# Scan of a hybrid flow step: attention's four scaled copies queued on ScalarE in written order, and the block inverse's conversions kept apart on ScalarE

## The chip, the cores and the metric

The kernel runs on one core of one Trainium2 chip, in one launch. The metric is device time in microseconds; the time before is the median of three runs. All instructions of the core are issued on five engines, each in its own order: TensorE (PE, with its weight loads PEld), VectorE (DVE), ScalarE (ACT), GpSimd (POOL) and SyncE (SP). Semaphores tie the engines together. DMAs are issued from the queues of SP, ACT and POOL.

## The reference, cut to what matters

One layer of a backbone for 128 context tokens and 2048 sample tokens, `D_MODEL` 1024. One input projection feeds three branches of 512 columns (a gated DeltaNet scan in both directions, a spatial gating MLP, a Fourier mix); each branch is gated, projected and merged.

```python
# the scan, chunk after chunk, forwards and backwards (H_A = 4 heads of 128)
m   = eye + beta * (k k^T) * dec_strict          # unit lower triangular, one per chunk and head
sol = solve_triangular(m, [beta v, beta exp(gam) k])
def step(s, inp):
    u = u0 - w @ s
    o = qg @ s + qk @ u                           # attention's output
    s = gl * s + kd^T @ u
    return s, o
# the branches
br  = stack([norm(o) * silu(z_a), sgu(u_b, v_b) * silu(z_b), fourier(x_c) * silu(z_c)])
merged = sum(sigmoid(gates) * (br @ w_branch)); y = rmsnorm(h + gate * (merged @ w_out))
```

## The kernel before, in words

All products are done in fp16 pairs (a high half and a low half, three matmuls for one product), so PE has most of the work: large products over 512 columns (`gemm_T`, `gemm_N`, line 250 with `xh`, `xl`, `whi`, `wlo`), and the small products of the scan, also through line 250. A weight block comes from HBM into `wst` (line 291), and becomes `wlo` with sums (line 315, ScalarE), `whi` (line 327, ScalarE) and a low half (line 328, VectorE); the tensors `blo` and `bhi` are the same for the branch projections.

The scan needs, for each chunk, the inverse of a triangular matrix. It is made in two parts. First come the inverses of the 32x32 diagonal blocks, for many chunks at once, in five groups (`base_inverse(g)`, lines 1092 to 1131, g from 0 to 4): the blocks come in as `XB` (line 1103, SyncE), then 31 elimination steps alternate between VectorE (line 1114, a product into `XB`) and GpSimd (line 1115, the subtraction into `E`), then `E` is converted to a pair of fp16 in four pieces (two halves of the columns, each once straight and once transposed): line 1122 on ScalarE gives the high half, line 1123 on VectorE the low half; after the two pieces of a half it goes out to `ei` by two DMAs. For g below 4 these DMAs are issued later from other places (lines 1003 and 1431); for g = 4 by SyncE and ScalarE themselves (lines 1130 and 1131). `XB` and `E` come from a pool with one buffer, so the next group's loads wait for the previous group's DMAs. After g = 4 the pool is closed and the scan's own loads begin (lines 1270 to 1322 and, for the levels, 1171 to 1177). Second, `level` (lines 1140 to 1226) builds a chunk's 128x128 inverse from its 32x32 blocks: loads of `ES` (line 1171) and `N` (line 1175), small products, and their conversions `Q` (lines 1184 to 1186 and 1218), `T` and `R` (line 1203).

The scan itself (`scan`, lines 1257 to 1360) runs over 17 chunks forwards, then 17 backwards. Each step multiplies with the state, forms `v16` and `u` (`split`, lines 1231 and 1232), and the new state's pair `S16`. `attend` (lines 1234 to 1255) forms the output: its first product goes into a PSUM bank of `ps_out`, is copied to `o` by four scaled copies, one per head, on ScalarE (line 1241), and the second product is added by VectorE (line 1248).

The scan and its preparation run beside the other branches. A pacing object hands out pieces of the delta branch between the large products. `gate_unit` of the other branches multiplies on GpSimd (line 1466, `st`), squares with a sum on ScalarE (line 1467, `sg`) and sends `st` out to `br` with a DMA issued on GpSimd (line 1468). `halves_of` (lines 1571 and 1572) makes the fp16 pairs of the Fourier branch (`xc`, `Y`). `big` (lines 1699 and 1700) makes the pair of a branch for the merge.

The order on each engine is not the written one. The program is recorded in written order, and a scheduler then moves instructions of each engine by priorities and by the times that it reckons. `A.queued()` (lines 187 to 191) returns a context that ties what is recorded in it behind the newest instruction recorded on that engine; what is tied so can't be scheduled ahead of it.

Of the kernel before, what the change touches and what calls it, by code (L numbers as in the profile page):

```python
# [14 lines left out]
AF = mybir.ActivationFunctionType  # L15
# [12 lines left out]
H = 4  # L28
# [7 lines left out]
FS = 4096.0  # L36
# [158 lines left out]
def hybrid_flow_kernel(ctx: ExitStack, tc: tile.TileContext, x_prompt, x_sample, state_delta, c, c_ctx, w_ada,  # L195
# [4 lines left out]
    G, V, A, PE = [_InTurn(tc, e_) for e_ in (nc.gpsimd, nc.vector, nc.scalar, nc.tensor)]  # L200
# [9 lines left out]
    def sb(pl, shape, tag, dt=F32, bufs=None):  # L210
        kw = {} if bufs is None else {"bufs": bufs}
        return pl.tile(list(shape), dt, tag=tag, name=nm(tag), **kw)
# [190 lines left out]
    def getw(n=1, ahead=0):  # L403
        i = wnext[0]
        wnext[0] += n
        fetch(i + n)
        while len(wdone) - len(wsteps) < i + n:
            weight_step()
        fetch(i + n + ahead)
        r = wdone[i:i + n]  # L410
        return r[0] if n == 1 else r
# [394 lines left out]
    beta, eg, egl, ed, neg = [sb(dp, dsh, n_) for n_ in ("beta", "eg", "egl", "ed", "neg")]  # L806
# [124 lines left out]
    for ct in range(12):  # L931
        w = getw(1, 2 if ct < 6 else min(4, 15 - ct))
        for half in range(1):
# [4 lines left out]
            for t0, tn in TBS:  # L938
                flip[0] ^= 1
                ps = bank(ps_d if flip[0] else ps_mm, [P, tn])  # L940
                gemm_T(ps, w, 0, xh[:, :, t0:t0 + tn], xl[:, :, t0:t0 + tn])
                o = t0 + 1 if t0 < NS else t0 + 3
# [32 lines left out]
    hs = lambda h: slice(h * P, (h + 1) * P)  # L975
# [116 lines left out]
    def base_inverse(g):  # L1092
# [25 lines left out]
        both = XB.bitcast(F16).rearrange("p (j l w c) -> p j l w c", j=32, l=2, w=2)  # L1118
        for j0 in (0, 16):
            js = slice(j0, j0 + 16)  # L1120
            for w, src in ((0, E3), (1, E.rearrange("p (i j) -> p j i", j=32))):
                A.activation(both[:, js, 0, w, :], src[:, js], AF.Copy, scale=FS)
                V.scalar_tensor_tensor(both[:, js, 1, w, :], src[:, js], FS, both[:, js, 0, w, :], ALU.mult, ALU.subtract)  # L1123
                yield 1
            out = [(eD[g][d][js].rearrange("j t (y x) -> (t y) j x", x=128),
                    both[64 * d:64 * d + nb, js].rearrange("p j l w c -> p j (l w c)")) for d in range(2)]
            if g < 4:
                extra.extend(out)
            else:
                SY.dma_start(*out[0])  # L1130
                A.dma_start(*out[1])
# [102 lines left out]
    def attend(d, t, S, u, qk_, qT_):  # L1234
        o = sb(dq, [P, WB], "o")
        if S is not None:
            ps = bank(ps_out, [P, WB])
            for h in range(H):
                mm3(ps[:, hs(h)], pair(qT_, h), pair(S, h))
            for h in range(H):  # L1240
                A.activation(o[:, hs(h)], ps[:, hs(h)], AF.Copy, scale=eg[:, d, t, h:h + 1])
        yield 1
        ps = bank(ps_out, [P, WB])
        for h in range(H):
            mm3(ps[:, hs(h)], pair(qk_, h), pair(u, h))
        if S is not None:
            for h in range(H):
                V.scalar_tensor_tensor(o[:, hs(h)], ps[:, hs(h)], rq[:, t, h:h + 1], o[:, hs(h)], ALU.mult, ALU.add)
        else:
            V.tensor_tensor(h3(o), h3(ps), bc(rq[:, t, :], P), ALU.mult)  # L1250
        yield 1
        if d == 0:
            SY.dma_start(ofD[t], o)
        else:
            yield from finish(t, o)
# [223 lines left out]
    ps = bank(ps_x, [P, 4, P])  # L1479
# [27 lines left out]
    for t in range(NCH):  # L1507
        ps = bank(ps_mm, [P, 4, P])
# [34 lines left out]
    for g in range(4):  # L1543
# [5 lines left out]
        for ti, (t0, tn) in enumerate(TBS):  # L1549
            st = vrow[:, t0:t0 + tn]  # L1550
            ps = bank(ps_mm, [P, tn])
# [26 lines left out]
    for g in range(4):  # L1578
        xw, zw = getw(2, 2)
        for gh in range(1):  # L1580
# [20 lines left out]
            for q in range(0, NCH, 4):  # L1601
                qn = min(4, NCH - q)
                ps = bank(ps_mm, [P, qn, P])
                for i in range(qn):
                    t = q + i
# [43 lines left out]
            for q4 in range(5):  # L1649
# [8 lines left out]
                if q4 == 2:  # L1658
                    ps = bank(ps_x, [P, P])
# [233 lines left out]
    ps = bank(ps_x, [P, 27])  # L1893
# [297 lines left out]
```

## Time and profile before

| what | value |
| --- | --- |
| median of three runs | 2145.91 us (2145.07 to 2146.69) |
| the profiled execution's own time | 2150.07 us |
| its span, from the first to the last instruction | 2148.3 us |
| mean granted TensorE clock | 0.992 |
| busy DVE, ACT, POOL | 1327.9, 1060.8, 843.3 us |
| first and last conversion of line 1122 | 548.1 and 881.0 us |
| first and last scaled copy of line 1241 | 942.0 and 1643.6 us |

Times of instructions are microseconds from the start of the span. The chain of waits is followed back from the last instruction, so what stands in it set the end. A row of waits gives an engine, its line and tile, what it waited for, the sum in us, the times and the longest wait. A row of windows gives busy time and instructions of each engine in a stretch, the granted clock of TensorE (1.00 is full speed), the DMA share and GB/s.

### The profile page before, as it was taken

The numbers are of one execution on the slowest core, as the hardware profiler recorded it, in microseconds if no ns is written. First come the engines' busy times: TensorE is split into PE (matmuls) and PEld (weight loads), VectorE is DVE, ScalarE is ACT, GpSimd is POOL, SyncE is SP. The second block draws the span as 40 slices with busy tenths as digits, with TensorE's granted clock in tenths as the row PEclk, the third lists the DMA queues.
The fourth block names the chain that finished last, engine by engine and source line by source line (L and its number), as shares of the span: only waits on it lengthen the run. The fifth ranks groups of instructions, "written<-read, shape, count | busy, mean of one in ns | idle before, by whom it ended". The sixth has DMA issues, their size and how long they took to land.

```text
span 2148.3 us, 42630 instructions
## 1 busy us (share of the span) xinstructions
PE 2085.2 (97%) x16133; PEld 1196.8 (56%) x16133; DVE 1327.9 (62%) x2945; ACT 1060.8 (49%) x2457; POOL 843.3 (39%) x1089
## 2 busy tenths in 40 slices
PE   7999999999999999989899999999999999999997
PEld 4454444455555677777555556565655444444443
DVE  6656854388777786456655555766665564666245
ACT  5554744475656664445544445665653353453112
POOL 0321332225565555542321233354542234333464
PEclk9999999999999999999999999999999999999999
DMA  9525722277877743444655555867664655456852
GB/s 353 219 77 189 267 102 102 74 223 226 259 228 246 225 138 93 121 132 138 205 182 161 167 162 184 258 206 232 210 204 127 209 167 173 167 198 240 335 220 89
DMA packets 222910, 403.25 MB, mean 188 GB/s; under 512 B 39720, under 2 KB 109632, under 8 KB 219888
## 3 DMA queue, kind: packets, MB, share of 16 engines
q1 hardware_dynamic: 167664, 290.84, 42.5%
q0 software_dynamic: 15216, 65.89, 8.2%
q10 hardware_dynamic: 39824, 43.79, 6.0%
q8 instruction: 127, 2.08, 0.4%
q14 instruction: 79, 0.65, 0.1%
HBM read 258.19 MB, written 142.24 MB: 186 GB/s over the span
## 4 chain that ended last, share of the span: by engine, by line
PE 70%; DVE 9%; DMA 9%; ACT 4%; POOL 4%; issue 3%; SPq 1%; ACTq 0%; DVEq 0%; POOLq 0%
PE b L250 66%; PE b L182 4%; DMA st<-br 2%; POOL E L1115 1%; DMA pa<-pa 1%; DMA wst<-in_w_blk_dram 1%; DVE XB L1114 1%; POOL st L1466 1%; DMA ab<-in_w_adb_dram 1%; PE b L1016 1%; DMA sqk<-qk 1%; DMA ei<-XB 0%; ACT xh L182 0%; ACT nd L1066 0%; DVE XB L1123 0%
## 5 line engine op out<-in xcount | busy, mean ns | idle before, releaser
L250 PE MATMUL b<-xh,whi 128*128 128x512 f16 (+1 forms) x1920 | 651.1, 348 | 2.8 <-DVE sg L1456 1.8
L250 PE MATMUL b<-xl,whi 128*128 128x512 f16 (+1 forms) x1920 | 651.2, 348 | 0.0
L250 PE MATMUL b<-xh,wlo 128*128 128x512 f16 (+1 forms) x1920 | 650.1, 347 | 0.0
L250 PEld LDWEIGHTS <-whi 128*128 128x128 f16 x3856 | 352.7, 98 | 326.4 <-issue 7.3
L250 PEld LDWEIGHTS <-wlo 128*128 128x128 f16 x1928 | 188.8, 98 | 176.1 <-issue 2.2
L250 PE MATMUL b<-big,bhi 128*128 128x512 f16 (+1 forms) x960 | 252.3, 347 | 1.9 <-ACT big L1699 1.1
L250 PE MATMUL b<-big,blo 128*128 128x512 f16 (+1 forms) x480 | 163.1, 347 | 0.0
L1743 POOL TENSOR_TENSOR mrow<-mrow,sg 128x512 f32<-128x512 f32 (+1 forms) x80 | 94.4, 1182 | 131.2 <-DVE sg L1742 99.5
L953 POOL TENSOR_TENSOR cy<-cy,raw 128x545 f32<-128x545 f32 (+1 forms) x48 | 65.8, 1395 | 181.8 <-ACT raw L952 181.8
L250 PEld LDWEIGHTS <-xh 128*128 128x128 f16 x1496 | 116.9, 98 | 28.8 <-issue 1.4
L250 PEld LDWEIGHTS <-bhi 128*128 128x128 f16 x960 | 87.7, 98 | 78.1 <-issue 2.6
L1115 POOL TENSOR_TENSOR E<-E,XB 128x31 f32<-128x31 f32 (+15 forms) x155 | 94.1, 607 | 85.7 <-DVE XB L1114 68.8
L250 PEld LDWEIGHTS <-xl 128*128 128x128 f16 x1068 | 98.1, 98 | 44.8 <-DMA tw<-tw 1.4
L1733 ACT ACTIVATE sg<-b,winv 128x512 f32<-128x512 f32 (+1 forms) x120 | 73.9, 616 | 87.1 <-PE b L250 86.4
L1188 POOL COPY T<-ES 32x256 f16<-32x256 f16 x68 | 31.8, 467 | 188.6 <-DMA ES<-ei 167.9
L250 PE MATMUL b<-whi,xh 128*128 128x128 f16 x544 | 92.8, 219 | 0.0
L250 PE MATMUL b<-whi,xl 128*128 128x128 f16 x544 | 92.8, 219 | 0.0
L250 PE MATMUL b<-wlo,xh 128*128 128x128 f16 x544 | 92.8, 219 | 0.0
L328 DVE SCALAR_TENSOR_TENSOR wlo<-wst,wsc,whi 128x1024 f16<-128x1024 f32 x52 | 71.1, 1368 | 33.1 <-ACT whi L327 32.7
L315 ACT ACTIVATE wlo<-wst 128x1024 f16<-128x1024 f32 x52 | 54.9, 1055 | 54.5 <-DMA wst<-in_w_blk_dram 51.2
L1114 DVE TENSOR_TENSOR XB<-XB,E 128x31 f32<-128x31 f32 (+15 forms) x155 | 55.2, 356 | 41.8 <-POOL E L1115 41.2
L1295 POOL TENSOR_TENSOR skn<-skn,ed 128x512 f32<-128x512 f32 x34 | 37.7, 1109 | 109.7 <-DMA skn<-kv 109.7
(532 smaller groups left out, 4317.9 us busy)
## 6 DMA issues: line engine op xcount, KB each, us to landing
wst<-in_w_blk_dram SPq DMA_DIRECT2D x58, 512.0 KB, 4.5
pa<-pa POOLq DMA_DIRECT2D x16, 896.0 KB, 4.4
qkv<-cy POOLq DMA_DIRECT2D x12, 1089.0 KB, 5.3
st<-br SPq DMA_DIRECT2D x48, 256.0 KB, 3.2
mrow<-mrg SPq DMA_DIRECT2D x16, 576.0 KB, 4.6
pa<-pa SPq DMA_DIRECT2D x5, 1792.0 KB, 17.3
dc<-dec SPq DMA_DIRECT2D x17, 512.0 KB, 4.8
kq<-qkv SPq DMA_DIRECT2D x34, 256.0 KB, 4.5
```

Source lines behind the costliest of these rows:

```text
L182: self.last = f(*args, **kw)
L250: newest[0] = PE.matmul(out, l, r, start=start, stop=stop, skip_group_check=reopened)
L315: w.squared = A.activation(w.lo, st, AF.Square, accum_out=ss)
L328: w.low = V.scalar_tensor_tensor(w.lo, st, s, w.hi, ALU.mult, ALU.subtract)
L953: G.tensor_tensor(y[:, c0:c1], y[:, c0:c1], raw[:, 1 + c0:1 + c1], ALU.mult)
L1016: PE.transpose(ps[:, hs(h)], cur[part][:, h, :], ident)
L1114: V.tensor_tensor(t3, X3[:, 0:k, k:k + 1].to_broadcast([P, k, n_]), E3[:, k:k + 1, k:32].to_broadcast([P, k, n_]), ALU.mult)
L1115: G.tensor_tensor(E3[:, 0:k, k:32], E3[:, 0:k, k:32], t3, ALU.subtract)
L1188: G.tensor_copy(T16[rows(a0, b), :, :, b], ES[0:32, :, 2 * a0 + b, :, wT])
L1295: G.tensor_tensor(h3(kn_), h3(kn_), bc(ed[:, d, t, :], P), ALU.mult)
L1733: gated_[0] = A.activation(sg, ps, AF.Sigmoid, scale=gw.inv)
L1743: G.tensor_tensor(mr, mr, sg, ALU.add)
```

## The change

Four conversions of each `base_inverse` are each recorded inside `A.queued()`, so each is tied behind the ScalarE instruction recorded just ahead of it (with the other engines' work of the generator between them: other parts of the program may record ScalarE work in between). The four scaled copies of an `attend` are recorded inside one `A.queued()`: all four are tied behind the same newest ScalarE instruction.

```diff
--- before.py
+++ after.py
@@ -1119,7 +1119,8 @@
         for j0 in (0, 16):
             js = slice(j0, j0 + 16)
             for w, src in ((0, E3), (1, E.rearrange("p (i j) -> p j i", j=32))):
-                A.activation(both[:, js, 0, w, :], src[:, js], AF.Copy, scale=FS)
+                with A.queued():
+                    A.activation(both[:, js, 0, w, :], src[:, js], AF.Copy, scale=FS)
                 V.scalar_tensor_tensor(both[:, js, 1, w, :], src[:, js], FS, both[:, js, 0, w, :], ALU.mult, ALU.subtract)
                 yield 1
             out = [(eD[g][d][js].rearrange("j t (y x) -> (t y) j x", x=128),
@@ -1237,8 +1238,9 @@
             ps = bank(ps_out, [P, WB])
             for h in range(H):
                 mm3(ps[:, hs(h)], pair(qT_, h), pair(S, h))
-            for h in range(H):
-                A.activation(o[:, hs(h)], ps[:, hs(h)], AF.Copy, scale=eg[:, d, t, h:h + 1])
+            with A.queued():
+                for h in range(H):
+                    A.activation(o[:, hs(h)], ps[:, hs(h)], AF.Copy, scale=eg[:, d, t, h:h + 1])
         yield 1
         ps = bank(ps_out, [P, WB])
         for h in range(H):
```

No instruction is added or taken away on any engine: the counts of each kind and shape are the same. What changes is the order, and not only of the tied instructions, since the scheduler places all others around them. Orders differ from about 548 us (the first group's conversions) to about 1200 us of the span, on all five engines; ahead of that and in the backward scan behind it they are the same. Lines below 1122 have one number more in the kernel after, those below 1241 two more. Three places follow.

The first is GpSimd (POOL) at the end of the last group, g = 4: `E_9690` and `XB_9689` are that group's tiles, `st` are gated pieces of other branches on their way to `br`. Before:

```order
L1115 TENSOR_TENSOR E_9690<-E_9690,XB_9689 128x4x28
L1466 TENSOR_TENSOR st_10527<-sg_10172,yT_9570 128x512
L1466 TENSOR_TENSOR st_10531<-sg_10231,yT_9570 128x512
L1466 TENSOR_TENSOR st_10535<-sg_10329,yT_9570 128x512
L1115 TENSOR_TENSOR E_9690<-E_9690,XB_9689 128x3x29
L1468 DMA br_3917<-st_10527 128x512
L1468 DMA br_3917<-st_10531 128x512
L1468 DMA br_3917<-st_10535 128x512
L1115 TENSOR_TENSOR E_9690<-E_9690,XB_9689 128x2x30
L1466 TENSOR_TENSOR st_10567<-sg_10564,yT_9570 128x512
L1466 TENSOR_TENSOR st_10599<-sg_10596,yT_9570 128x128
L1115 TENSOR_TENSOR E_9690<-E_9690,XB_9689 128x31
```

And after the change, the same stretch:

```order
L1115 TENSOR_TENSOR E_9690<-E_9690,XB_9689 128x4x28
L1115 TENSOR_TENSOR E_9690<-E_9690,XB_9689 128x3x29
L1468 TENSOR_TENSOR st_10527<-sg_10172,yT_9570 128x512
L1468 TENSOR_TENSOR st_10531<-sg_10231,yT_9570 128x512
L1468 TENSOR_TENSOR st_10535<-sg_10329,yT_9570 128x512
L1115 TENSOR_TENSOR E_9690<-E_9690,XB_9689 128x2x30
L1470 DMA br_3917<-st_10527 128x512
L1470 DMA br_3917<-st_10531 128x512
L1470 DMA br_3917<-st_10535 128x512
L1115 TENSOR_TENSOR E_9690<-E_9690,XB_9689 128x31
```

The elimination steps of 3, 2 and 1 columns (128x3x29, 128x2x30 and 128x31) have moved: the first ahead of the three products of line 1466, the second ahead of the three DMA issues, the last ahead of the two products that follow those.

The second place is ScalarE (ACT) just behind it, where that group is converted; `sg` are the squares of line 1467 and `ei` is where the inverses go. Before:

```order
L1571 ACTIVATE xc_10704<-b_10607 128x512
L1467 ACTIVATE sg_10564,oss_431_3920<-st_10567 128x512
L1467 ACTIVATE sg_10596,oss_431_3920<-st_10599 128x128
L1122 ACTIVATE XB_9689<-E_9690 128x16x32 x4
L1571 ACTIVATE xc_10826<-b_10711 128x512
L1131 DMA ei_3930<-XB_9689 64x16x128 x2
L1571 ACTIVATE Y_1289_10604<-b_10829 128x64x8
```

After:

```order
L1573 ACTIVATE xc_10704<-b_10607 128x512
L1123 ACTIVATE XB_9689<-E_9690 128x16x32 x2
L1469 ACTIVATE sg_10564,oss_431_3920<-st_10567 128x512
L1469 ACTIVATE sg_10596,oss_431_3920<-st_10599 128x128
L1132 DMA ei_3930<-XB_9689 64x16x128
L1123 ACTIVATE XB_9689<-E_9690 128x16x32 x2
L1573 ACTIVATE xc_10826<-b_10711 128x512
L1573 ACTIVATE Y_1289_10604<-b_10829 128x64x8
L1132 DMA ei_3930<-XB_9689 64x16x128
```

The four conversions, which stood together behind the two squares, are now two ahead of the squares and two behind them, with the first DMA between.

The third place is ScalarE in the forward scan between its fourth and fifth set of attention's copies (about 1024 to 1034 us before): `blo` reads a weight block that arrives by DMA as `wst`, `S_1545` is the state's pair for the next step, `kn` its keys. Before:

```order
L1454 ACTIVATE sg_13384<-b_13283,winv_11212 128x512
L1467 ACTIVATE sg_12888,oss_431_3920<-st_13260 128x512
L1454 ACTIVATE sg_13417<-b_13391,winv_11212 128x128
L1467 ACTIVATE sg_13047,oss_431_3920<-st_13279 128x512
L327 ACTIVATE bhi_13449<-wst_11441,wsc_13456 128x512
L1297 CAST kn_1551_13567<-skn_13541 128x512
L1231 ACTIVATE S_1545_13524<-S_11074 128x512
L315 ACTIVATE blo_13798,bsums_93<-wst_13634 128x512
```

After:

```order
L1456 ACTIVATE sg_13384<-b_13283,winv_11212 128x512
L327 ACTIVATE bhi_13449<-wst_11441,wsc_13456 128x512
L1469 ACTIVATE sg_12788,oss_431_3920<-st_13256 128x512
L1456 ACTIVATE sg_13417<-b_13391,winv_11212 128x128
L1469 ACTIVATE sg_12888,oss_431_3920<-st_13260 128x512
L1299 CAST kn_1551_13567<-skn_13541 128x512
L315 ACTIVATE blo_13798,bsums_93<-wst_13634 128x512
L1469 ACTIVATE sg_13047,oss_431_3920<-st_13279 128x512
L1232 ACTIVATE S_1545_13524<-S_11074 128x512
```

The conversion `bhi` has moved ahead of two squares, and `blo`, which stood behind the state's pair, now stands ahead of it and of one square.

Two more moves, told in words: the fourth set of attention's copies (`o_13238`, begun at 1009.81 us before) stood ahead of the level's `Q` conversions (lines 1184, 1186 and 1218) and now stands behind them; the sixth set (begun at 1043.43 us before, in the midst of the conversions to `big` of line 1699) now stands behind the last of those (1077.26 us before).

## Prediction

> **What bounds the kernel now.** I read the page first, then the windows of the stretch in which the order differs, then what TensorE (PE) waits for there, then the chain of waits. From the page, the busy time of the engines and the chain by engine:
>
> ```profile
> PE 2085.2 (97%) x16133; PEld 1196.8 (56%) x16133; DVE 1327.9 (62%) x2945; ACT 1060.8 (49%) x2457; POOL 843.3 (39%) x1089
> PE 70%; DVE 9%; DMA 9%; ACT 4%; POOL 4%; issue 3%; SPq 1%; ACTq 0%; DVEq 0%; POOLq 0%
> ```
>
> PE is busy for 97% of the span, and no PE instruction is removed. So the change can only act on PE's idle time and on its granted clock, and only where the order differs, 548 to about 1200 us. The windows there (busy us of PE, PEld, DVE, ACT, POOL; then the granted clock):
>
> ```profile
> 760.00:870.00 110.00, 105.14 (x1242) 80.72 (x1240) 80.30 (x199) 54.18 (x142) 58.18 (x93) 0.98 0.33 103
> 870.00:980.00 110.00, 100.37 (x1499) 85.83 (x1497) 59.78 (x141) 52.12 (x123) 50.85 (x78) 0.95 0.50 143
> 980.00:1090.00 110.00, 101.14 (x1000) 65.60 (x998) 73.94 (x192) 59.89 (x143) 36.18 (x57) 0.95 0.58 178
> 1090.00:1200.00 110.00, 110.00 (x1009) 65.40 (x1007) 63.12 (x173) 48.36 (x111) 24.13 (x41) 1.00 0.54 165
> ```
>
> From 1090 PE has no gap at full clock: nothing to win there, only to lose. In the two windows from 870 to 1090 PE idles for 110 - 100.37 = 9.6 and 110 - 101.14 = 8.9 us, and the clock of 0.95 costs another 110 x 0.05 = 5.5 us in each. In shorter windows the low clock lies right at the idle time:
>
> ```profile
> 900.00:920.00 20.00, 14.86 (x120) 8.93 (x121) 7.90 (x19) 6.17 (x18) 8.57 (x16) 0.81 0.34 103
> 1020.00:1040.00 20.00, 15.98 (x164) 11.18 (x162) 13.41 (x40) 12.24 (x32) 12.65 (x16) 0.88 0.50 159
> ```
>
> So the sum has four terms: the scan's start near 900, the clock there, and the attention copies and the other moves between 1009 and 1080.
>
> **Term 1, the scan's start.** What PE waits for between 890 and 920 (total us, times, longest):
>
> ```profile
> PE b L250 <- DMA ES<-ei: 2.5, 1, 2.5
> PE b L250 <- DMA N<-n: 1.9, 1, 1.9
> PE b L250 <- ACT Q L1186: 1.0, 1, 1.0
> PE b L250 <- ACT R L1203: 0.5, 1, 0.5
> PE b L250 <- ACT xc L1571: 0.4, 1, 0.4
> ```
>
> That is 6.3 us. The chain of waits leads from there back to the last group's conversions:
>
> ```profile
> 879.10 1.52 ACT XB L1122 x2
> ...
> 883.33 5.41 DMA ei<-XB
> ...
> 892.30 6.46 DMA sqk<-qk
> ...
> 911.25 2.66 DMA ES<-ei
> ```
>
> The scan's loads queue on SyncE behind the outgoing inverses, and their landing is what PE awaits. So what counts is how early the four conversions of g = 4 and their DMAs are done. GpSimd there before (start, us, operation):
>
> ```profile
> 870.29 3.75 POOL L1466 TENSOR_TENSOR st<-sg,yT 128x512 f32<-128x512 f32 x3 [0.54 <-DVE yT L1642]
> 873.99 0.36 POOL L1115 TENSOR_TENSOR E<-E,XB 128x87 f32<-128x87 f32 x1
> 874.28 1.65 POOL L1468 DMA_DIRECT2D br<-st  x3
> 875.96 0.32 POOL L1115 TENSOR_TENSOR E<-E,XB 128x60 f32<-128x60 f32 x1
> 876.78 1.68 POOL L1466 TENSOR_TENSOR st<-sg,yT 128x512 f32<-128x512 f32 x2 [0.51 <-DMA br<-st]
> 878.42 0.25 POOL L1115 TENSOR_TENSOR E<-E,XB 128x31 f32<-128x31 f32 x1
> ```
>
> After the change the 87-element step goes ahead of the 3.75 us of products, the 60-element step ahead of the 1.65 us of DMA issues, the last ahead of the 1.68 us. With VectorE's product for it ready at about 870.5 (an estimate: it has two pieces of `yT` to do until 870.2), I get 870.5 + 0.36 + 3.75 = 874.6, then 0.32 and 1.65 to 876.55, and the last step ends at 876.8 instead of 878.67: **1.9 us earlier**. ScalarE before:
>
> ```profile
> 878.08 0.63 ACT L1467 ACTIVATE sg<-st 128x512 f32<-128x512 f32 x1 [1.64 <-POOL st L1466]
> 878.71 0.29 ACT L1467 ACTIVATE sg<-st 128x128 f32<-128x128 f32 x1
> 879.00 3.12 ACT L1122 ACTIVATE XB<-E 128x512 f16<-128x512 f32 x4
> ```
>
> Two conversions now run at 876.8 to 878.4, in time in which ScalarE idled (1.64 us in the row above). The other two wait behind the squares, these for the products on GpSimd, these for a `br` DMA to free their buffer (0.51 us idle in GpSimd's row). That DMA is now issued 874.9 - 874.28 = 0.6 us later, so the squares end at about 879.6 instead of 879.0. Conversions three and four then end at 881.2 instead of 882.1: **0.9 us earlier**. The first half goes out some 2 us earlier and shares less of the queue with the second.
>
> The group before, g = 3, has the same shape: its last two steps pass the three products of line 1466, and three of the four conversions go ahead of two squares. The fourth stands behind these two, which wait for `br` again. Its chain:
>
> ```profile
> 817.72 2.03 ACT XB L1122 x3
> ...
> 823.32 5.18 DMA ei<-XB
> ...
> 829.29 5.19 DMA XB<-nd
> ```
>
> The first half leaves some 3 us earlier (an estimate: the 3.75 us that three such products took in the row of g = 4, less what ScalarE has queued ahead), the second at about the same time (-0.5 us, its low half on VectorE no longer queued behind three others), and the loads of the next `XB`, which wait for both DMAs, pass a weight load on SyncE. I take 1.2 us, between 0 (the fourth conversion holds it all) and 2.5. Everything from there to 870 alternates between VectorE and GpSimd, so it is handed on: the scan starts 0.9 + 1.2 = 2.1 us earlier. PE's own work ahead of the waits has moved by under 2 us either way. Of the 6.3 us some 2 go for the start, and about 1 more since `Q` of line 1186 is now queued ahead of other conversions: **-3 us**. Bounds: all 6.3 gone; or 2 more, if less of PE's filler now lies in front of the waits.
>
> **Term 2, the clock.** 900 to 920 at 0.81 is 20 x 0.19 = 3.8 us lost. The low clock stands only where stalls cluster, so fewer stalls should shorten it, but not in proportion: beside 20 - 14.86 = 5.1 us of idle time stand 3.8 us lost, beside 20 - 15.98 = 4.0 us only 20 x 0.12 = 2.4. I take half: **-1.9 us**, with bounds of -3.8 (gone) and +3.8 (a second such stretch).
>
> The Trainium skill (TensorE: Matmul & The Clock Gate, HAM oscillation — how this bites in real kernels) gives as a rule "no PE-idle gaps >~3.4µs". By that rule no wait listed here, 2.5 us at most, would lower the clock, and shorter ones would not raise it; term 2 would be 0. The row of 0.81 speaks against it as a strict bound: a cluster of short waits has the low clock too.
>
> **Term 3, the attention copies.** Both kinds of copies, by line (ns minimum, median, maximum):
>
> ```profile
> L1122 ACT ACTIVATE XB<-E x20: 612/846/1112, 548.1 to 881.0; 128x512 f16<-128x512 f32 x20
> L1241 ACT ACTIVATE o<-b,eg x128: 347/367/403, 942.0 to 1643.6; 128x128 f32<-128x128 f32 x128
> ```
>
> Four copies are a block of some 1.15 us on ScalarE. PE's waits from 1010 to 1080:
>
> ```profile
> PE b L250 <- DVE Q L1219: 1.7, 1, 1.7
> PE b L250 <- DVE o L1248: 1.7, 2, 1.3
> PE b L250 <- ACT u L1231: 1.5, 1, 1.5
> PE b L250 <- ACT big L1699: 1.1, 2, 0.7
> PE b L250 <- ACT Q L1186: 1.1, 2, 0.6
> PE b L250 <- DVE S L1232: 0.7, 1, 0.7
> ```
>
> The fourth set no longer stands ahead of `Q`: of 1.1 us for line 1186 I count 0.6 gone. The sixth set goes back behind `big`, and PE's products with `u` move behind other work: of 1.5 us I count 0.7. The late sets hold a bank of `ps_out`, so their second product comes later; nothing waits for it but the output's DMA. **-1.3 us**, bounds -2.6 and 0. If that cover is gone (the bank is needed), a block of four, 1.15 us, is paid once.
>
> **Term 4, what pays.** ScalarE before, in the third place shown of the change:
>
> ```profile
> 1030.49 0.63 ACT L1231 ACTIVATE S<-S 128x512 f16<-128x512 f32 x1 [1.37 <-DVE S L1345]
> 1032.65 0.63 ACT L315 ACTIVATE blo<-wst 128x512 f16<-128x512 f32 x1 [1.52 <-DMA wst<-in_w_brb_dram]
> ```
>
> `blo` waits for a DMA, and now stands ahead of the state's pair. With that DMA landing at 1032.6 as before, the pair would begin at 1032.65 + 0.63 + a square of 0.63 = 1033.9, 3.4 us late, and with it the scan's next product. But `bhi`, behind whose buffer the load waits, also moved ahead of two squares, about 2 us; so 1.4 us is left. PE has other work for part of it (S line 1232 is awaited for 0.7 us only). I take **+0.7**, and +0.8 for `big` (1.1 us of waits on ScalarE alone now), whose conversions move by 2 to 5 us while the products that use them move less: **+1.5 us**, bounds 0 and 3.4 + 2 = 5.4, with 2.4 us on top for a second stretch at the 0.88 of 1020 to 1040.
>
> From 548 to 870 I count nothing: PE idles 4.9 us in 760 to 870, the orders shift by 1 to 2 us both ways.
>
> **The sum.** -3 - 1.9 - 1.3 + 1.5 = -4.7 us. The profiled execution took 2150.07 us, so one like it would take 2145.4. The median of the runs is 4.2 us below that execution, and on it the sum gives 2145.9 - 4.7 = **2141 us**.
>
> **The rivals.**
>
> *No change.* The change says that the conversions are kept apart, but only ties each behind what was recorded ahead of it; two (or one) still stand behind the squares, and these behind a `br` DMA. If the second half's landing comes no earlier, terms 1 and 2 are 0, and -1.3 + 1.5 leaves 2146. Against it: the first half leaves earlier in any case. The rule on the clock ends in the same place: with term 2 at 0 the sum is -2.8, 2143 us, within 0.2%; the 0.81 of the row makes it no more than one chance in ten, counted in this rival.
>
> *Slower by head-of-line blocking on ScalarE.* The state's pair waits behind `blo`. If the load comes no earlier, the chain of states is late by 3.4 us, `big` adds 2, and the clock stretch at 1020 to 1040 repeats: 2.4 more. Together +7.8; with 2 us of term 1 left, +5.8, 2152 us. It decides from the point at which PE runs out of other work, about 1.4 us of lateness. For it: PE already waits there for `Q`, `o` and `S`. Against it: between 1090 and 1200 PE idles not at all, so a late chain is caught up where PE has work in stock; it then costs only what PE idles before.
>
> **How the numbers follow.** A measurement of this kernel can tell about 0.2% from no change, 4.3 us. The forecast, faster, has 0.43, no change 0.29, slower 0.28. The forecast itself is close to the bound, so it gives its own range as 2134 to 2143. The lower end of all is -6.3 - 3.8 - 2.6 = -12.7, 2133 us; the upper one term 4 at its end with the clock, 7.8 us above the median, 2154 us.
>
> **What would show it.** Right: the last conversion of g = 4 (881.0 before) begins at about 880; the waits for `ES` and `N` after 890 together under 3 us; the clock of 900 to 920 above 0.9; copies of line 1241 (1243 after) not awaited by PE; the span below 1220 shifted by some 5 us. Wrong: the `ei` DMAs land no earlier, or new waits of more than 2 us for `S`, `big` or `Q` between 1020 and 1090, or a clock below 0.95 there. If the backward scan behind 1220 changes in length, then something is at work that I have not named.

## The result, and the profile after

The changed kernel takes 2154.59 us (median of four runs, 2152.47 to 2158.68), the kernel before 2145.55 us on the same chip: a ratio of 1.0045, 95% interval [1.0028, 1.0062], slower by some 9 us. In a second comparison, with 11 executions of the changed kernel and 35 of the one before instead of four each, the same pair gave 1.0018 [1.0006, 1.0029], some 4 us. Slower both times; the forecast was 5 us faster, its own range 2134 to 2143, and the end of all ranges 2154. The executions of one kernel differ by several us here (35 of the kernel before: 2141.82 to 2156.14), so what follows goes by intervals and by places in the traces. The profiled execution after took 2155.19 us, its span is 2153.4 us.

The changed kernel's page, the busy time of the engines and the chain:

```profile
PE 2086.8 (97%) x16133; PEld 1197.9 (56%) x16133; DVE 1334.8 (62%) x2945; ACT 1062.5 (49%) x2457; POOL 841.5 (39%) x1089
PE 47%; DVE 6%; DMA 6%; ACT 3%; POOL 2%; issue 2%; SPq 0%; ACTq 0%; DVEq 0%; POOLq 0%
```

The engines have the same instructions as before. The windows of the changed stretch, after (columns as before):

```profile
760.00:870.00 110.00, 103.73 (x1214) 80.49 (x1212) 79.38 (x194) 53.65 (x141) 58.84 (x90) 0.97 0.34 101
870.00:980.00 110.00, 101.37 (x1551) 86.69 (x1549) 62.65 (x147) 54.05 (x126) 50.49 (x82) 1.00 0.50 144
980.00:1090.00 110.00, 100.18 (x989) 64.49 (x987) 74.64 (x189) 60.65 (x141) 34.86 (x56) 0.97 0.58 179
1090.00:1200.00 110.00, 110.00 (x1014) 65.98 (x1012) 62.12 (x175) 47.70 (x109) 25.77 (x42) 1.00 0.51 162
```

From 870 to 980 PE idles less and has its full clock, as forecast; it does 1551 matmuls there instead of 1499. But 760 to 870, which was counted at nothing, has 1.4 us more idle time and a lower clock. In windows of 20 us, the first two rows before, the others after:

```profile
820.00:840.00 20.00, 20.00 (x323) 18.26 (x321) 10.62 (x22) 8.16 (x16) 4.47 (x11) 1.00 0.52 123
840.00:860.00 20.00, 18.87 (x161) 11.55 (x160) 15.08 (x39) 6.75 (x16) 12.71 (x21) 1.00 0.08 28
```

```profile
820.00:840.00 20.00, 17.13 (x296) 16.96 (x294) 7.05 (x15) 6.49 (x12) 4.19 (x9) 0.96 0.59 131
840.00:860.00 20.00, 19.89 (x150) 11.97 (x148) 14.75 (x39) 6.98 (x16) 11.78 (x20) 0.95 0.08 27
900.00:920.00 20.00, 15.50 (x148) 9.05 (x147) 10.62 (x26) 9.83 (x24) 7.68 (x16) 1.00 0.45 127
1020.00:1040.00 20.00, 16.09 (x178) 11.40 (x177) 13.56 (x36) 12.74 (x32) 12.66 (x16) 0.91 0.43 141
```

The low clock of 900 to 920 (0.81 before) has gone, and another stands at 820 to 860. What PE waits for from 820 to 850 in the changed kernel, in one row:

```profile
PE b L250 <- DVE xc L1574: 2.9, 1, 2.9
```

VectorE there, after (start, us, operation, and in brackets the idle time ahead and its cause):

```profile
827.94 1.28 DVE L328 SCALAR_TENSOR_TENSOR wlo<-wst,wsc,whi 128x1024 f16<-128x1024 f32 x1 [0.96 <-ACT whi L327]
836.50 1.03 DVE L1107 COPY XB<-XB 64x1024 f32<-64x1024 f32 x1 [7.27 <-DMA XB<-nd]
837.56 0.69 DVE L1574 SCALAR_TENSOR_TENSOR xc<-b,xc 128x512 f16<-128x512 f32 x1
```

**The first place.** The copy that opens group 4's inverse (line 1107) waits 7.3 us for its load, and the Fourier conversion `xc`, which PE needs, is queued behind it. Before, VectorE waited there too, but `xc` and the `Y` behind it stood ahead of the copy, which began 2.0 us earlier:

```profile
834.50 1.05 DVE L1107 COPY XB<-XB 64x1024 f32<-64x1024 f32 x1 [3.97 <-DMA XB<-nd]
```

The prediction didn't look at VectorE's order here. It shows the swap; before:

```
L328 SCALAR_TENSOR_TENSOR wlo_9675<-wst_8991,wsc_9812,whi_9674 128x1024
L1572 SCALAR_TENSOR_TENSOR xc_9915<-b_9818,xc_9915 128x512
L1572 SCALAR_TENSOR_TENSOR Y_1213_9571<-b_9918,Y_1213_9571 128x64x8
L1107 COPY XB_9689<-XB_9689 64x1024
```

and after: `wlo`, then the copy, then `xc`, an elimination product, and `Y`.

The load is late as well. The chain of the changed kernel, with ScalarE's DMA issue and its last conversion of group 3:

```profile
820.47 1.83 ACTq L1003
...
823.36 0.99 ACT XB L1123
...
826.18 5.19 DMA ei<-XB
...
836.50 1.05 DVE XB L1107
```

The last elimination step of group 3 ended at 811.1, and its fourth conversion at 824.3: 13.3 us, where before it was 3.3 (817.5 to 820.7). The third conversion stands behind squares that wait for GpSimd's products, and begins at 817.7; the two DMA issues and two more squares stand between it and the fourth.

**The last group.** ScalarE after, where the four conversions stood in one block before:

```profile
880.89 1.60 ACT L1123 ACTIVATE XB<-E 128x512 f16<-128x512 f32 x2
882.58 0.63 ACT L1469 ACTIVATE sg<-st 128x512 f32<-128x512 f32 x1
...
883.45 0.31 ACT L1469 ACTIVATE sg<-st 128x128 f32<-128x128 f32 x1
...
884.26 0.61 ACTq L1132 DMA_DIRECT2D ei<-XB  x1
884.91 1.62 ACT L1123 ACTIVATE XB<-E 128x512 f16<-128x512 f32 x2 [1.06 <-DVE XB L1124]
```

The DMA of the first half waits for VectorE's low half, and ScalarE stands still for 1.06 us until it has issued it. With this and the two squares between, the fourth conversion ends 5.8 us behind the last elimination step (880.7 to 886.5); before it was 3.45 (878.67 to 882.12). The scan's first waits of PE from 890 to 920, after:

```profile
PE b L250 <- POOL T L1189: 2.6, 1, 2.6
PE b L250 <- DVE Q L1220: 1.0, 1, 1.0
PE b L250 <- DMA ES<-ei: 0.4, 1, 0.4
PE b L250 <- POOL X L1628: 0.3, 1, 0.3
PE b L250 <- ACT Q L1187: 0.2, 1, 0.2
```

4.5 us instead of 6.3. PE itself came 4.7 us late (the weight sum of line 315 that began at 896.02 before begins at 900.71). The first loads of `ES` were issued 4.2 us late (899.08 instead of 894.89), and the wait behind them is no shorter: 2.6 us for `T`, which the chain follows back to these loads, where before 1.9 us went for `N`. The next loads of `ES` were issued only 1.4 us late (911.84 instead of 910.41), and there the wait fell from 2.5 to 0.4 us.

**The second place.** PE's waits from 1010 to 1080, after, and ScalarE behind them:

```profile
PE b L250 <- ACT S L1232: 1.7, 1, 1.7
...
PE b L250 <- DVE S L1233: 1.3, 1, 1.3
PE b L250 <- DVE Q L1220: 1.2, 1, 1.2
...
PE b L250 <- ACT Q L1187: 0.5, 1, 0.5
```

```profile
1032.29 0.63 ACT L315 ACTIVATE blo<-wst 128x512 f16<-128x512 f32 x1 [1.65 <-DMA wst<-in_w_brb_dram]
...
1032.92 0.61 ACT L1469 ACTIVATE sg<-st 128x512 f32<-128x512 f32 x1
...
1033.53 0.61 ACT L1232 ACTIVATE S<-S 128x512 f16<-128x512 f32 x1
```

The state's pair begins at 1033.53 instead of 1030.49, behind `blo` and a square, as the second rival had it. PE waits 3.0 us for the pair, 0.7 before. The wait for `u` went, and those for `Q` became shorter (lines 1187 and 1220 are 1186 and 1219 before: 0.5 and 1.2 us instead of 1.1 and 1.7). All waits of PE from 1010 to 1080 together are 8.9 us, 8.7 before.

**Where the difference of the two profiles lies.** For the instructions of five lines of ScalarE (315, 1454, 1467, 1571, 1733; 474 of them) I took the start after minus the start before, and the median in a stretch. After is 1.5 us late at 700 to 795, 5.3 at 834 to 845, 0.0 at 990 to 1012, 1.0 at 1165 to 1230, and 5.4 at 1720 to 1900. So what was lost near 835 was made good by 1000 in this pair of executions, and 4.4 us were lost in the backward scan, where the order is that of before (a low clock at 1596, 0.91 from 1580 to 1620). One pair of profiles therefore can't say what the 9 us are, and the execution that is compared with counts too: a second profile of the kernel before (`e4` below) gains 2.1 us against the first between 860 and 1000.

### The profile page after: what moved, and what is told of

Same layout as the page of the kernel before. It is cut to its first block, busy times and chain, and to the rows that moved or that the text cites. A ratio compares the mean times of both kernels' runs of the same rounds, so it can differ in the third digit from the quotient of the medians.

```text
span 2153.4 us, 42632 instructions
## 1 busy us (share of the span) xinstructions
PE 2086.8 (97%) x16133; PEld 1197.9 (56%) x16133; DVE 1334.8 (62%) x2945; ACT 1062.5 (49%) x2457; POOL 841.5 (39%) x1089
## 4 chain that ended last, share of the span: by engine, by line
PE 47%; DVE 6%; DMA 6%; ACT 3%; POOL 2%; issue 2%; SPq 0%; ACTq 0%; DVEq 0%; POOLq 0%
PE b L250 46%; DMA st<-br 2%; DMA wst<-in_w_blk_dram 1%; DMA tw<-tw 1%; POOL E L1115 1%; DVE XB L1114 1%; DMA ei<-XB 0%; ACT big L1701 0%; DVE big L1702 0%; DMA ES<-ei 0%; PE b L1384 0%; DVE XB L1124 0%; POOL st L1468 0%; DVE wlo L328 0%; ACT nd L1066 0%
## 5 line engine op out<-in xcount | busy, mean ns | idle before, releaser
L1744 DVE SCALAR_TENSOR_TENSOR sg<-b,binv,sg 128x512 f32<-128x512 f32 (+1 forms) x80 | 53.4, 669 | 42.8 <-PE b L250 39.0
```

The source lines that it names most:

```text
L1744: V.scalar_tensor_tensor(sg, ps, binv[:, 1:2], sg, ALU.mult, ALU.mult)
```

## The experiments

Each ratio is to the kernel before on the same chip, with its 95% interval; the median of before was 2145.7 to 2147.5 us, so 0.0010 is 2.1 us.

### The two parts, and both kernels again

`e1` queues only the conversions, `e2` only attention's copies; `e3` and `e4` are the kernels after and before, unchanged.

> Only the block inverse's conversions are queued; attention's copies are as before. Theory A (VectorE is blocked near 830: its copy of line 1107, which waits for the next group's load, now stands ahead of a Fourier conversion that PE needs): the wait of PE for that conversion, 2.9 us in the changed kernel at 835, and the low clock behind it are there again, PE's work near 870 is some 4 us late, and it is made good by 990; the time against before is 0 to +3 us. Theory B (the loss behind 1220, where the order on every engine is that of before, is drawn anew in each run by the clock and the DMAs): +3 to +7 us, with the loss behind 1220. Theory C (the loss is the attention copies'): 0 us within 1.

Measured: 1.0019 [1.0006, 1.0032], that is 4.1 us, above theory A's 0 to +3 and within B's +3 to +7. The wait at 835 is there (2.5 us). C falls, since there is a loss; B's place is not borne out (behind 1230 this execution took 0.5 us less than the first profile of before).

> Only attention's four copies are queued; the conversions are as before, and so is all order up to about 940 us. Theory A: nothing at 835, so no loss of 4 us there; against before 0 to +4 us. Theory B: +3 to +7 us, with the loss behind 1220. Theory C: +7 to +10 us, as the whole change.

Measured: 1.0008 [0.9996, 1.0021]. No wait at 835, and one of 2.1 us for the state's pair near 1030.

> The changed kernel once more, for a second profile and more times. Theory A: the wait of PE at 835 of 2.9 us and the low clock at 838 are there again, +7 to +10 us. Theory B: the wait at 835 too, but the low clock and the losses behind 1220 lie at other places than in the first profile; the times spread over 4 us or more. Theory C: as A, with the same late places from 1009 to 1165.

Measured: 1.0018 [1.0006, 1.0029]. The wait at 835 again (2.8 us), a wait of 3.1 for the pair; behind 1230 it lost nothing this time (-0.3 us). At 1.0018, 3.9 us, theories A and C (+7 to +10) both miss. So the 4.4 us of the first profile in the backward scan belong for the most part to that execution. A low clock from 1580 to 1620 stands here too, though (0.96), and again in `e10` (0.96), and in none of the other profiles; whether the change has a part in it isn't shown.

> The kernel before once more, for a second profile: 0 us within 1.5. Theory B says that its low clock stretches lie elsewhere than in the first profile and that it too can lose 2 us or more behind 1220 in some runs; theories A and C say that the stretch behind 1220 takes as long as in the first profile, within 1 us.

Measured: 1.0000 [0.9990, 1.0011]. Between 795 and 1000 this execution was 3.0 us faster than the first profile of the same kernel, and 1.9 behind 1230: theory B is right that single executions differ so, wrong that it explains the times.

### The first place alone

`e5` ties VectorE's copy behind what stood ahead of it before, in the whole change:

```diff
-        with V.queued():
+        with V.queued(), tc.issue_after(low[0].ins) if g == 4 else ExitStack():
             V.tensor_copy(b3(X[64:P, :]), tmp[64:P, :].rearrange("p (i j) -> p j i", j=32))
...
     def halves_of(hi, lo, src, scale):
...
-        V.scalar_tensor_tensor(lo, src, scale, hi, ALU.mult, ALU.subtract)
+        low[0] = V.scalar_tensor_tensor(lo, src, scale, hi, ALU.mult, ALU.subtract)
```

> The whole change, with one tie more: VectorE's copy of line 1107 of the last group stands behind the low halves of the Fourier branch that were recorded ahead of it, as it stood in the kernel before. Theory A (the loss is VectorE's wait near 830, 3.7 us of PE's lateness from there on): the 2.9 us wait of PE at 835 and the low clock at 838 are gone, PE's work at 850 is within 1 us of before, and the time is 3 to 4 us less than the changed kernel's, 0 to +2 us against before. Theory D (what is lost near 830 is made good by 990 in any case, the loss is elsewhere): the stall goes too, but the time stays at +5 us against before.

Measured: 1.0024 [1.0016, 1.0033], 5.1 us. The wait did not go, it moved. PE's waits from 830 to 850 with the tie:

```profile
PE b L250 <- DVE xc L1576: 2.5, 1, 2.5
```

The two conversions that the tie names went ahead, and the next `xc` now stands behind the copy and six elimination products (begun at 839.08). So `e5` is no clean removal: the time is theory D's, but the stall, which both theories had going, is still there, and theory A could neither stand nor fall by it.

`e6` leaves group 2 out of the change, `e7` queues only group 2:

```diff
-                with A.queued():
+                with A.queued() if g != 2 else ExitStack():
```

> The whole change but for the four conversions of group 2 (near 700 us), which are not queued. The order on VectorE near 830 is then that of before. Theory A: no wait of PE at 835; as with attention's copies alone, 0 to +3 us against before. Theory D: +5 us, as the whole change.

Measured: 1.0023 [1.0011, 1.0034]. No wait from 820 to 850 at all, and still 5 us slower, theory D's number and above theory A's 0 to +3: the first place isn't the whole cost.

> The kernel before, with only the four conversions of group 2 queued. On VectorE the copy of line 1107 of the last group and three elimination products then stand ahead of the Fourier conversion that PE waits for. Theory A: a wait of PE near 835 of 4 us or more with a low clock behind it, PE's work at 850 late by 4 to 7 us, +3 to +7 us against before at the end. Theory D: the same near 835, but 0 to +1.5 us at the end.

Measured: 1.0011 [1.0000, 1.0023]. Four conversions near 700 us, and nothing else, turn VectorE's order 130 us later. PE's waits from 820 to 880 were

```profile
PE b L250 <- DVE sg L1457: 2.0, 1, 2.0
PE b L250 <- DVE xc L1573: 1.4, 1, 1.4
```

and the last elimination step ended at 869.7 instead of 878.7, with the first product of the scan at 893.4 instead of 901.1. The scan began 8 us earlier, and the kernel was not faster: 2.4 us slower, between the ranges of theories A and D. That is a blow to term 1 as a whole, though no clean price for an early start, since the waits above may have taken some of it back.

### The split of the last conversions

`e8` queues attention's copies and groups 3 and 4, `e9` groups 3 and 4 alone (`if g >= 3 else ExitStack()` in both); `e10` is the whole change with ScalarE's two issues written behind the loop:

```diff
             else:
                 SY.dma_start(*out[0])
-                A.dma_start(*out[1])
+                halves.append(out[1])
+        for o_ in halves:
+            A.dma_start(*o_)
```

> Attention's copies and only the conversions of groups 3 and 4 are queued; all else is ordered as with attention's copies alone, so GpSimd's and VectorE's order near 810 to 890 is that of before. It shows what splitting the last group's conversions brings by itself. By the recorded prediction's term 1 the inverses would leave up to 1 us earlier than before; by theories A and D nothing changes for them that reaches the end: as with attention's copies alone, 0 to +3 us against before, no wait at 835.

Measured: 1.0029 [1.0016, 1.0042], 6.2 us, with no wait at 835 and one of 2.9 us for the pair near 1030. The upper end of what was expected was 3.

> The kernel before, with only the conversions of groups 3 and 4 queued. On PE, VectorE and ScalarE together 24 positions differ from before, on GpSimd and SyncE none; so this is the split of the last conversions alone. Theory E (splitting them delays them: ScalarE's squares and its DMA issue, which waits for VectorE's low half, come between): the fourth conversion ends 4.1 us behind the last elimination step for group 3 (3.3 before) and 5.3 for group 4 (3.5 before), the scan's first load is issued 2 to 3 us later, and the time is +2 to +4 us. Theory F (the scan's start does not set the end): the same in the conversions, but 0 us within 1.5 at the end.

Measured: 1.0000 [0.9989, 1.0010]: theory F. The split does delay: ScalarE in `e9`

```profile
877.41 1.59 ACT L1123 ACTIVATE XB<-E 128x512 f16<-128x512 f32 x2
...
880.75 1.61 ACT L1123 ACTIVATE XB<-E 128x512 f16<-128x512 f32 x2 [0.56 <-issue]
```

puts the fourth's end 5.3 us behind the last elimination step (3.5 before); the time does not show it.

> The whole change, with the two DMA issues that ScalarE does for the last group written behind all four conversions instead of one behind each half. All four conversions of group 4 then stand together, ahead of the two squares. Theory E: the fourth ends 3.3 to 3.7 us behind the last elimination step instead of 5.8, the scan's loads begin 2 us earlier than in the changed kernel, and the time is 1.5 to 3 us below the changed kernel's. Theory F: the same, but the time stays at the changed kernel's, +4 to +5 us against before.

Measured: 1.0026 [1.0014, 1.0037]. The four stand together again, and the fourth ends 3.3 us behind the last step:

```profile
879.92 3.11 ACT L1124 ACTIVATE XB<-E 128x512 f16<-128x512 f32 x4
```

The time stays. F again.

### The sets of attention's copies

Of the sets, only the first, the fourth and the sixth change any order when queued alone. `e11` and `e12`:

```diff
+            sets[0] += 1
-            with A.queued():
+            with A.queued() if sets[0] == 4 else ExitStack():
```

> The kernel before, with only the fourth set of attention's copies queued (near 1010 us); this alone puts the load's conversion blo ahead of the state's pair, and the sixth set behind some conversions to big. Theory G (the attention part costs by the late state's pair): a wait of PE for the pair of 2 to 3 us near 1030 instead of 0.7, the wait for the pair of Q near 1009 at 1.2, and +1 to +3 us at the end. Theory H (what the attention copies do is made good by 1100, when PE has work in stock): the same waits, but 0 us within 1.5 at the end.

Measured: 1.0017 [1.0005, 1.0029], and in `e18` below 1.0011 [0.9996, 1.0026].

> The kernel before, with only the sixth set of attention's copies queued (near 1043 us); order differs only from there to about 1200 us. Theory G: no late state's pair near 1030, so 0 us within 1.5, or less by the wait for u of 1.5 us near 1078 that goes. A wait for the copies of 1 us or more near 1072 to 1084 would put up to +2 us on it. Theory H: 0 within 1.5.

Measured: 0.9993 [0.9982, 1.0005]. PE's waits from 1020 to 1042, `e11` ahead of `e12`:

```profile
PE b L250 <- ACT S L1231: 2.9, 1, 2.9
...
PE b L250 <- DVE S L1232: 0.5, 1, 0.5
```

```profile
PE b L250 <- DVE Q L1219: 1.6, 1, 1.6
PE b L250 <- DVE o L1252: 1.3, 1, 1.3
PE b L250 <- DVE S L1232: 0.7, 1, 0.7
...
```

The fourth set brings the late pair and a loss (its second measurement, `e18`, doesn't exclude 0), the sixth brings neither.

### Without the fourth set, and without both places

`sets[0] != 4` in attention alone (`e13`), in the whole change (`e14`), in `e8` (`e15`), and in `e5` (`e16`).

> Attention's copies queued but for the fourth set; the conversions are as before. Theory G (of the attention part, the fourth set costs, since the state's pair then waits behind blo): no wait of PE for the pair above 1 us near 1030, and -3 to +0.5 us against before. Theory H (no set costs by itself): +1 to +3 us, as with all sets.

Measured: 0.9992 [0.9980, 1.0005].

> The whole change but for the fourth set. Theory I (the cost is the sum of two places: VectorE's wait for the last group's load near 835, and the late state's pair near 1030): the wait at 835 stays, that for the pair goes, and the time is +1 to +3.5 us against before. Theory J (any of these orders costs some 5 us, since each is off the order before; no place counts by itself): +4 to +6 us.

Measured: 1.0018 [1.0005, 1.0031], 3.9 us, between theory I's +3.5 and theory J's +4. Two waits for Fourier conversions are left from 825 to 850, none of over 1 us for the pair:

```profile
PE b L250 <- DVE xc L1577: 3.6, 2, 2.2
```

> Attention's copies but for the fourth set, and the conversions of groups 3 and 4. With all sets this cost +6.2 us. Theory I: neither place is left, so -2 to +1.5 us. Theory J: +4 to +6 us.

Measured: 0.9999 [0.9987, 1.0012], against 1.0029 with the fourth set; the two intervals lie apart. PE still waits 2.3 us for the pair near 1030 in this profile (1.6 and 0.7), though ScalarE makes it ahead of `blo`: here a wait of that size for the pair cost nothing.

> The whole change, with VectorE's copy tied behind the Fourier conversions and without the fourth set. Theory I: both places are lighter, 0 to +2.5 us. Theory J: +4 to +6 us.

Measured: 1.0004 [0.9991, 1.0017], against 1.0024 with the fourth set. The wait for `xc` from 825 to 850 is 2.2 us, less than in `e14`, but not gone.

Theory J falls with `e13`, `e15` and `e16`: orders far from that of before cost nothing there.

### Which move of the fourth set

`e17` is `e11` with one tie, which puts `blo` behind the state's pair again; `e18` is `e11` once more, on the same chip:

```diff
-        with behind_gate():
+        blos[0] += tag == "b"
+        with behind_gate(), tc.issue_after(pairs[-1].ins) if tag == "b" and blos[0] == 2 else ExitStack():
             w.squared = A.activation(w.lo, st, AF.Square, accum_out=ss)
```

(`pairs` holds the state's pairs of `split`.)

> The fourth set alone queued, with one tie more: blo's sum (line 315) stands behind the state's pair again, as before. Theory G (the late pair is what the fourth set costs): the wait of PE for the pair near 1030 falls from 2.9 us to about 0.7 and the time from +3.3 us to -1 to +1 us against before. Theory K (the other moves of the fourth set cost: Q behind, the sixth set behind some conversions to big): the wait falls too, but the time stays at +2 to +4 us.

Measured: 1.0004 [0.9991, 1.0017], median 2147.05 us.

> The fourth set alone once more, on the same chip as the run with the tie: a wait of 2.9 us for the pair near 1030, and +2 to +4 us against before, by both theories.

Measured: 1.0011 [0.9996, 1.0026], median 2149.95 us. Three windows of `e18`, then of `e17`:

```profile
1000.00:1020.00 20.00, 17.98 (x231) 14.39 (x229) 13.23 (x41) 8.89 (x26) 6.52 (x14) 0.91 0.49 142
1020.00:1040.00 20.00, 15.79 (x170) 11.30 (x168) 14.97 (x42) 12.25 (x32) 11.86 (x16) 0.85 0.50 151
1040.00:1060.00 20.00, 18.83 (x112) 9.00 (x110) 12.26 (x29) 12.91 (x25) 4.99 (x8) 0.89 0.75 243
```

```profile
1000.00:1020.00 20.00, 17.98 (x245) 13.92 (x244) 14.31 (x44) 9.93 (x28) 8.19 (x17) 1.00 0.48 140
1020.00:1040.00 20.00, 14.81 (x177) 9.94 (x175) 16.94 (x42) 14.54 (x39) 10.36 (x13) 1.00 0.64 195
1040.00:1060.00 20.00, 18.30 (x129) 9.56 (x128) 12.98 (x29) 11.91 (x22) 6.37 (x9) 1.00 0.76 252
```

In the profile with the tie the low clock is not there, and the idle time is (`e17` idles even longer from 1020 to 1040, but does more matmuls). PE's wait for the pair is 1.5 us, not the 0.7 that was expected, against 2.8 in `e18`, and a load of `qT` is awaited for 1.4 us. The tie also changed the order of other ScalarE work from 1035 to 1080. The medians are 2.9 us apart as theory G has it, but the two intervals overlap. Over their twelve executions (span times one minus the mean clock) `e17` lost 17.5 us to the clock and `e18` 20.1, so all of the difference between them can be the clock. `e17` points to theory G and doesn't show it.

### What the runs say together

The stretch from about 1000 to 1200 us, by the method at the end of the section on the result (change of lateness against the first profile of before, in us):

| kernels | change from 990-1012 to 1165-1230 | mean |
| --- | --- | --- |
| with the fourth set: after, e2, e3, e5, e6, e8, e10, e11, e18 | 1.0, 0.9, 3.8, 4.9, 6.1, 5.3, 3.8, 1.2, 4.1 | 3.5 |
| without it, or with the pair first: before, e1, e4, e7, e9, e12 to e17 | 0, -1.0, 0.3, 1.3, -0.2, -1.5, 0.4, 1.1, -1.3, -0.1, -1.1 | -0.2 |

So **the fourth set costs about 3.6 us between 1000 and 1200** on the mean; single executions scatter, and three of the nine with it lie among those without. In the windows from 1000 to 1100 of the same profiles, the kernels of the first row have 10.7 us of PE's idle time and 6.6 us lost to the low clock on the mean, those of the second 9.2 and 3.9: the low clock has more of the cost than the waits. By times, all but the last across comparisons, the fourth set is worth 0.0030 (`e8` and `e15`), 0.0020 (`e5` and `e16`), 0.0016 (`e2` and `e13`) and 0.0011 to 0.0017 alone, that is 2.4 to 6.4 us. In the whole change the pair `e3` and `e14`, 1.0018 both, doesn't show it; `e14` against the first measurement of the change, 1.0045, does. Which of the set's moves costs, the pair behind `blo` or another, is not shown.

The conversions cost where groups 0 to 2 are among them (`e1` 1.0019, `e14` 1.0018, `e7` 1.0011), and nothing with groups 3 and 4 alone (`e9` 1.0000, `e15` 0.9999). All of the first kind have the wait near 835 for a Fourier conversion behind VectorE's copy, the second kind has not.

The lateness shows the place: from 700-795 to 850-870 the eight kernels with that wait (after, `e1`, `e3`, `e5`, `e7`, `e10`, `e14`, `e16`) fall back by 2.5 us on the mean (1.5 to 3.3), the eight with the order of before there (before, `e2`, `e4`, `e11` to `e13`, `e17`, `e18`) by -0.5 (-1.0 to 0.5), and `e6`, which leaves out group 2 alone, by -0.2. With groups 3 and 4 alone it is -0.6 and 0.1 (`e9`, `e8`), and 2.0 in `e15`, whose clock was 0.83 from 800 to 820. That is **about 3 us for the first place by 870**. From there to 990-1012 the two kinds gain the same on the mean (3.2 and 3.1 us), so it isn't made good there. That it reaches the end is the likeliest reading of the times, and `e16` against `e14` (1.0004 and 1.0018, with a wait of 2.2 instead of 3.6 us) points to it, but their intervals overlap, and no run took the wait wholly away with the rest kept. **That stays open**. So does why the parts don't add up: in the second comparison the whole change cost no more than one of the two places alone, while `e8`, made of parts worth 1.0008 and 1.0000, cost 1.0029.

`e12` and `e13` lie below before at 0.9993 and 0.9992, and neither interval excludes no change. No version here is shown to be faster than the kernel before.

## Why the prediction was wrong

- **What bounds it.** Right: PE's work is unchanged, and only idle time and clock move.
- **Term 1, GpSimd's steps.** Right, and nearly in size: from the 112-element step's end to the last one's it took 7.4 us (873.3 to 880.7) instead of 8.9 (869.7 to 878.7), 1.6 less where I had 1.9; but PE, and all behind it, came so late that the last step ended 2.0 us later. **Term 1, the conversions: wrong.** The step that said "conversions three and four then end at 881.2 instead of 882.1" left out ScalarE's own DMA issue that the order showed between them. It waits for VectorE's low half, and the conversions wait for it: the fourth conversion ends 5.8 us behind the last step, where the forecast had 4.4 (876.8 to 881.2) and the kernel before 3.45. So the split took back 2.4 us, more than the 1.6 that the steps brought; for group 3 it was 13.3 instead of 3.3. The rival *no change* had the two conversions behind the squares, not behind the issue.
- **Term 1, what an earlier scan is worth: wrong.** `e7` began the scan 8 us earlier and `e9` delayed its conversions by 1.8 us, and the time was 1.0011 and 1.0000. The waits of 6.3 us were real, but what was gained or lost there didn't reach the end; that PE's filler work and later waits took it up is likely and not shown.
- **Group 3 to 870, "handed on", and "from 548 to 870 I count nothing": wrong.** Group 4's copy began 2.0 us later (836.50), not 1.2 earlier. Near 830 the change swapped it with the Fourier conversion PE needs; 2.9 us of wait and a low clock made PE 3.8 us late in this profile, and the place costs about 3 us by 870 over all of them, where I had put 0. I had read ScalarE, GpSimd and SyncE there and not VectorE.
- **Term 2.** Right at its place (1.00 from 900 to 920, in `e3` too), but the low clock came up elsewhere (0.96 and 0.95 from 820 to 860), and the windows from 1000 to 1100 above have more of it with the fourth set. Nor does it stand "only where stalls cluster": before, 800 to 820 had 0.92 with PE busy for all 20.00 us, 1040 to 1060 0.87 with 19.04. Over the whole span the cost isn't a slower clock alone: `e3`'s eleven executions average 19.4 us lost (span times one minus the mean clock), before's 35 of that job 20.1; `e5` lost 21.3 and `e8` 20.4, before in their job 18.6.
- **The signs of terms 1 and 2 came true without them.** `ES` and `N` were awaited for 0.4 us after 890 and the clock was 1.00 from 900 to 920, as for a right forecast; but PE had come 4.7 us late, and the last conversion began at 885.4, not at 880.
- **Term 3.** Of 1.1 us for `Q` of line 1186, 0.6 went, as counted, and the wait for `u` went. All waits from 1010 to 1080 together stayed the same (8.9 us, 8.7 before), since those for the pair and `big` grew. By `e12`, the sixth set brings nothing that can be told from 0.
- **Term 4: the place right, the size wrong.** The +0.7 for the state's pair behind `blo` stood for a move that the fourth set brings, and that set cost about +3.6 (the mean of the table; the forecast's own upper estimate for the pair was 3.4). The pair did come 3.0 us late; that this move alone is the cost is likely and not shown. I took most of it as hidden by other work, since `S` was waited for only 0.7 us before; but a wait that is short before says nothing of how much work is in stock. The +0.8 for `big` was right (1.8 us of waits before, 2.6 after). The rival *slower by head-of-line blocking* named the place and, with 5.8 to 7.8 us, about the price.
- **The range.** Its lower end adds the bounds of terms 1, 2 and 3; its upper end, 2154, takes term 4 with the clock alone and leaves out the forecast's own bounds of +2 for term 1 and +3.8 for term 2. With them it would have ended near 2160.
- **The rule of the Trainium skill (TensorE: Matmul & The Clock Gate, HAM oscillation — how this bites in real kernels), "no PE-idle gaps >~3.4µs".** No wait of PE from 820 to 860 in the changed kernel was longer than 2.9 us, none from 1000 to 1060 in `e18` longer than 2.3, and the clock fell to 0.95 and 0.85 in windows there. The rows speak against it as a strict bound, as they did before.

## What to carry to other kernels

A tie on one engine gives a scheduler a reason to place other work anew on all of them: read the order of every engine down to the stretch where it agrees again, above all where an instruction that waits for a DMA changes places with one that PE needs. An instruction that issues a DMA counts as work and as a wait on the engine that issues it, as ScalarE's row with 1.06 us shows. A wait that was short before doesn't price the same wait made longer.

## What the runs showed of the hardware

ScalarE can stand still for a DMA that it issues itself: 1.06 us behind a low half of VectorE in the last group, and 3.13 us ahead of a square at 822.35 in group 3, of which the chain puts 1.83 us down to the issues of line 1003. And executions of one kernel differ by more than the change: with the same order throughout, 990 to 1012 us was reached 3.0 us earlier, counted from 795, in the second profile of the kernel before than in the first, and the low clock from 900 to 920 was at 0.83 and 0.81 in the two.
